# Two mixture-of-experts layers: routing from unscaled rows, modulation on VectorE, three index lists moved behind a branch

## Chip, cores and metric

The kernel runs on one core of a Trainium2 chip. The metric is the device time of one execution in microseconds; a time of several executions is given as their median.

## What is computed

The reference takes 512 tokens of 1024 floats through two blocks. The first has two layers of latent attention beside dilated attention. The second has two layers, each a mixer (attention with pooling in the first, a gated convolution in the second) and a mixture of 16 experts; each token goes to 2 of them, chosen within one of four groups. The change touches the mixture alone. Cut to what matters:

```
h = rms_norm(x, g) * (1 + scale) + shift            # "modulate"
group = top1(softmax(h @ rg_w + rg_b))
two   = top2(softmax(h @ re_w + re_b) within the group)
for e in 16 experts:
    y += weight[e] * (silu(h @ w_gate[e]) * (h @ w_up[e])) @ w_down[e]
x = x + g2 * y
```

## The kernel before

The 512 tokens lie as four tiles `x[:, i, :]` of 128 rows. `moe` is called once a layer and has four stretches.

**Routing.** The output projection of the mixer before it leaves eight half tiles of `x` open; `arrive` draws one: six matmuls (L350 to L352) and an addition on VectorE (L1037). Between them the list in the first scheduled section draws `square` (ScalarE, the sum of squares), `scaled` (L1571, `y = x * A`), `turned` (L1544, eight transpositions of `y` on TensorE, copied out by ScalarE), `logits` and `folded` (L1552, L1558), `rms` (the inverse root, a chain of one-column operations on VectorE, L384 to L397) and `modulate` (`y * rs + shift`, stored to the scratch tensor `tscr`). VectorE does `modulate` in one operation (L1582); GpSimd's form takes a scaling on ScalarE and an addition on GpSimd (L1585). Tiles 0 and 1 go to GpSimd, 2 and 3 to VectorE. `route` ranks the logits of one tile on VectorE (L1591 to L1611); `before` and `spots` turn the choice into positions within each expert.

**Index lists.** `hot` compares positions with a ramp on VectorE (L1631, tile `oh`, two buffers), `places` multiplies it with the row numbers on TensorE (L1637, L1642), `indices` adds the parts up (L1648, `ix`). `place(0, 1)` makes the list of expert 0, `place(1, 3)` those of experts 1 to 3. `fetch` (L1670) gathers the 128 rows of one expert from `tscr` with an indirect transfer that GpSimd issues.

**The branch.** A register is loaded from `over` (L1880), and every engine branches on it (L1881). The body is a loop over all experts for lists of over 128 tokens. With these inputs it isn't entered: the trace has no instruction of L1885 to L1926. Each engine passes a short other branch that waits for what stands before it on its own counters.

**Experts.** An expert multiplies the turned rows (`turn`, L1747, eight transpositions) with 1 MB of gate and up weights. Each product is three matmuls of two halves of 32 bits (`xTh`, `xTl`, `whi`, `wlo`): `split_to` makes the upper half on ScalarE (L401), the lower on VectorE or GpSimd (L402). A chunk `c1` of the weights (1024 columns) takes six matmuls, an expert 24; `hidden` (L1762) follows them, `down` the second product. `split0` makes chunks 0 to 2 of expert 0 ahead of the expert, on GpSimd. `weigh` works out the weight of each token from the logits (L1683 to L1722, 21 small operations on VectorE and two on ScalarE). `up(1)` follows `up(0)`, then the second place of `info` with the weights, then `down(0)`.

Within `manual_schedule` TensorE, GpSimd, ScalarE and VectorE take their instructions in the order in which the list is written; a scheduler lays other work between.

Of the kernel before, what the change touches and what calls it, by code (L numbers as in the profile page):

```python
# [1487 lines left out]
def router(k, L):  # L1488
# [7 lines left out]
    for c in range(8):  # L1496
# [4 lines left out]
TABLES = ("mv", "iota", "tri", "info", "rw", "fold")  # L1501
SMALL = ("lg", "sm", "cmp", "rank", "G", "lgr", "gm", "ge", "gsum", "e2", "w1", "w2", "sec", "We", "Ws",
         "Ab", "pos", "pos16", "most", "over", "oh", "row", "spread", "lgT", "ix", "ws", "vinf", "vpos", "ivx", "ivw",
# [13 lines left out]
def moe(k, L, x, tables, out):  # L1517
# [4 lines left out]
    A, sh, g2B, iota, tri, info, rw, fold = tables  # L1522
# [15 lines left out]
    def turned(i, qs=(0, 1)):  # L1538
        src = ys[i]
        tT = tTs[i] = xgs[i].rearrange("p (c t) -> p c t", c=8)  # L1540
        for q in qs:
            pt = k.bank("pt")
            for j in range(4):
                nc.tensor.transpose(pt[:, j * P : (j + 1) * P], src[:, (4 * q + j) * P : (4 * q + j + 1) * P], ident)  # L1544
            nc.scalar.activation(tT[:, 4 * q : 4 * q + 4, :], pt.rearrange("p (k t) -> p k t", k=4), AF.Copy)
# [18 lines left out]
    def square(i):  # L1564
        nc.scalar.activation(xgs[i], x[:, i, :], AF.Square, scale=float(D ** -0.5), accum_out=ss[:, i : i + 1])
# [4 lines left out]
    def scaled(i, engine, cs=slice(0, D)):  # L1570
        engine.tensor_tensor(ys[i][:, cs], x[:, i, cs], A[:, cs], ALU.mult)  # L1571
# [8 lines left out]
    def modulate(i, engine, cs=slice(0, D)):  # L1580
        if engine is v:
            v.scalar_tensor_tensor(ys[i][:, cs], ys[i][:, cs], rss[i], sh[:, cs], op0=ALU.mult, op1=ALU.add)  # L1582
        else:
            nc.scalar.activation(ys[i][:, cs], ys[i][:, cs], AF.Copy, scale=rss[i])
            engine.tensor_tensor(ys[i][:, cs], ys[i][:, cs], sh[:, cs], ALU.add)  # L1585
        if cs.stop == D:
            nc.sync.dma_start(tscr[i * P : (i + 1) * P, :], ys[i])
# [195 lines left out]
    with tc.manual_schedule(engines={ENG.PE, ENG.Pool, ENG.Activation, ENG.DVE}):  # L1783
        k.arrive()
        square(0)
        scaled(0, v)
        k.arrive()
        square(1)
        scaled(1, nc.gpsimd)
        k.arrive(1)  # L1790
        run(rms(0, 2))
        turned(0)
# [32 lines left out]
        for i in range(2):  # L1825
            before(i)
# [268 lines left out]
```

## Time and profile before

| | us |
|---|---|
| median of three runs (lowest, highest) | 1857.73 (1855.89, 1859.37) |
| the profiled execution | 1858.75 |
| its span from first to last instruction | 1857.0 |
| TensorE busy | 1705.9 (92%) |
| VectorE busy | 1346.4 (73%) |
| ScalarE busy | 770.8 (42%) |
| GpSimd busy | 278.2 (15%) |

Times in the rows are microseconds from the span's start. In the first layer of experts routing runs from 1226.5 to about 1260, the experts to about 1445. In the second routing runs from about 1625 to 1659, the experts to about 1845. The rest of the span is the attention block and the two mixers, which the change leaves as they are.

### The profile page before, as it was taken

Reading aid. Unit: us, or ns where it says so; the run is one execution under the profiler, and the core shown is the slowest. Engines: PE = TensorE matmul, PEld = TensorE weight load, DVE = VectorE, ACT = ScalarE, POOL = GpSimd, SP = SyncE. Lnnn points to the kernel's source line nnn. Section 1 sums busy time; section 2 is a strip of 40 time slices with the busy share of each in tenths; the row PEclk is TensorE's granted clock in tenths of the full one; section 3 lists DMA queues with packets and bytes.
Section 4 is the critical chain, followed back from the end, with each engine's and each line's share of the span. In section 5 each row is a group of like instructions: output and inputs, shape, how many; then the busy total and the mean of one; then the engine's idle time right before and its main releaser. Section 6 shows DMA issues by size and latency. Waiting matters only on the chain. (4 is left out here: it accounts for less than half of the span.)

```text
span 1857.0 us, 25754 instructions
## 1 busy us (share of the span) xinstructions
PE 1705.9 (92%) x9542; PEld 1334.2 (72%) x9542; DVE 1346.4 (73%) x2532; ACT 770.8 (42%) x1345; POOL 278.2 (15%) x242
## 2 busy tenths in 40 slices
PE   7999999999799999999997889987999799969996
PEld 7877777886697777778866767765666587746663
DVE  4577778876646777576677788879877765589774
ACT  4444333333343443323434445553555322145552
POOL 0000000001200000000003452023221122142221
PEclk9999999999999999999998989997999799979998
DMA  5345565664024445554413213147996463169983
GB/s 176 121 135 149 162 206 162 192 193 135 19 73 125 142 143 151 169 165 148 150 46 110 67 47 126 42 170 265 336 341 194 164 215 95 36 247 304 348 295 75
DMA packets 86948, 298.90 MB, mean 161 GB/s; under 512 B 18854, under 2 KB 20694, under 8 KB 78624
## 3 DMA queue, kind: packets, MB, share of 16 engines
q1 hardware_dynamic: 71584, 271.87, 43.8%
q0 software_dynamic: 10704, 19.79, 4.7%
q10 hardware_dynamic: 4528, 5.51, 1.1%
q8 instruction: 78, 1.28, 0.3%
q14 instruction: 54, 0.44, 0.1%
HBM read 280.23 MB, written 24.96 MB: 164 GB/s over the span
## 5 line engine op out<-in xcount | busy, mean ns | idle before, releaser
L401 ACT ACTIVATE whi<-wraw 128x1024 fp32r<-128x1024 f32 (+2 forms) x166 | 171.7, 1036 | 348.1 <-PE psmm L351 241.6
L350 PE MATMUL psmm<-big,whi 128*128 128x512 f32 x672 | 272.9, 406 | 6.8 <-DVE x L668 5.6
L402 DVE TENSOR_TENSOR wlo<-wraw,whi 128x1024 fp32r<-128x1024 f32 (+3 forms) x165 | 200.9, 1219 | 102.3 <-ACT whi L401 89.6
L352 PE MATMUL psmm<-big,wlo 128*128 128x512 f32 x672 | 266.7, 397 | 0.0
L351 PE MATMUL psmm<-big,whi 128*128 128x512 f32 x672 | 266.6, 397 | 0.0
L980 DVE CUSTOM_DVE_ANT_0 wraw<-wraw,sB 128x1024 f32<-128x1024 f32 x96 | 117.1, 1221 | 83.4 <-DMA wraw<-in_mw_dram 82.9
L350 PE MATMUL psmm<-whi,big 128*128 128x256 f32 (+2 forms) x496 | 165.1, 333 | 1.5 <-ACT big L401 1.0
L351 PE MATMUL psmm<-wlo,big 128*128 128x256 f32 (+2 forms) x496 | 160.7, 324 | 4.9 <-DVE wlo L402 4.9
L352 PE MATMUL psmm<-whi,big 128*128 128x256 f32 (+2 forms) x496 | 159.9, 323 | 2.4 <-DVE big L402 2.3
L350 PEld LDWEIGHTS psmm<-big,whi 128*128 128x128 f32 x672 | 127.3, 189 | 35.8 <-issue 4.7
L352 PEld LDWEIGHTS psmm<-big,wlo 128*128 128x128 f32 x672 | 126.9, 189 | 31.1
L351 PEld LDWEIGHTS psmm<-big,whi 128*128 128x128 f32 x672 | 127.4, 190 | 27.9
L1865 PE MATMUL psmm<-wraw,hs 128*128 128x512 f32 x256 | 122.1, 619 | 5.4 <-ACT hs L1857 3.5
L601 POOL DMA_DIRECT2D qk<-rope x40 | 20.5, 515 | 659.2 <-ACT whi L401 286.9
L351 PEld LDWEIGHTS psmm<-wlo,big 128*128 128x128 f32 x496 | 112.1, 226 | 6.2 <-DVE wlo L402 6.0
L352 PEld LDWEIGHTS psmm<-whi,big 128*128 128x128 f32 x496 | 111.5, 225 | 3.2 <-DVE big L402 3.2
L350 PEld LDWEIGHTS psmm<-whi,big 128*128 128x128 f32 x496 | 111.4, 225 | 2.7 <-ACT big L401 1.7
L350 PE MATMUL pss<-whi,xTh 128*128 128x512 f32 x256 | 104.8, 409 | 2.4 <-ACT xTh L401 2.4
L352 PE MATMUL pss<-whi,xTl 128*128 128x512 f32 x256 | 102.4, 400 | 1.7 <-DVE xTl L402 1.7
L351 PE MATMUL pss<-wlo,xTh 128*128 128x512 f32 x256 | 103.4, 404 | 0.0
L856 PEld LDWEIGHTS pspt<-c_ident,pr 128*128 128x128 f32 x512 | 61.3, 143 | 48.2 <-issue 28.9
L402 DVE TENSOR_TENSOR wlo<-bigm,whi 128x1024 fp32r<-128x1024 f32 x64 | 77.9, 1223 | 17.7 <-ACT whi L401 16.2
(384 smaller groups left out, 3659.7 us busy)
## 6 DMA issues: line engine op xcount, KB each, us to landing
wraw<-in_mw_dram SPq DMA_DIRECT2D x96, 512.0 KB
big<-in_me_dram SPq DMA_DIRECT2D x32, 1024.0 KB
bigm<-in_me_dram SPq DMA_DIRECT2D x32, 1024.0 KB
wraw<-in_me_dram SPq DMA_DIRECT2D x64, 512.0 KB
wraw<-in_wqk_dram SPq DMA_DIRECT2D x48, 512.0 KB
wraw<-in_wv_dram SPq DMA_DIRECT2D x24, 512.0 KB
wraw<-in_ow_dram SPq DMA_DIRECT2D x20, 512.0 KB
wraw<-in_wg_dram SPq DMA_DIRECT2D x16, 512.0 KB
```

Source lines behind the costliest of these rows:

```text
L350: mm(out, lhs[0], rhs[0], start=first, stop=False)
L351: mm(out, lhs[0], rhs[1], start=False, stop=False)
L352: mm(out, lhs[1], rhs[0], start=False, stop=last)
L401: self.nc.scalar.activation(hi, src, AF.Copy)
L402: (sub or self.nc.vector).tensor_tensor(lo, src, hi.bitcast(F32), ALU.subtract)
L601: nc.gpsimd.dma_start(tiles[b][48:80, :], R[b // 4][32 * (b % 4) : 32 * (b % 4) + 32, :])
L856: nc.tensor.transpose(pt[:, j * P : (j + 1) * P], hd.pr[i][:, j * P : (j + 1) * P], ident)
L980: nc.vector.tensor_tensor_reduce(w, w, sB, 1.0, 0.0, ALU.mult, ALU.add, mf[:, j : j + 1])
L1865: nc.tensor.matmul(acc, hs[:, c * P : (c + 1) * P], w[:, c * 512 : (c + 1) * 512], start=c == 0, stop=c == 1)
```

## The change

- The router's weights are scaled once (`cols`, a new small load, and one operation on VectorE), so that `turned` takes its transpositions from `x` itself and no longer from `y`.
- `scaled` and `modulate` run on VectorE alone. The tiles are modulated in the order 0, 3, 2, 1: 0 and 3 ahead of `route` of tiles 0 and 1, 2 and 1 between that and `route` of tiles 2 and 3. The squares of tile 3 are summed in two halves.
- The three `split0` go from GpSimd to VectorE and behind the branch. The scheduler lays the first of them ahead of routing.
- `place(1, 3)` and the fetch of expert 1 go from ahead of the branch to behind it. `turn`, two splits and then all of `weigh` follow.
- Two runs of idle transpositions, `warm(8)` ahead of the last two `route` and `warm(24)` between the fetch of expert 0 and the branch.
- The loads within the body of the branch go from SyncE's queue to GpSimd's.

```diff
-    tables = [brow(k, rows[L], j, ("mv", 3)) for j in (4, 3, 5)]
+    cols = small([P, 8], "cols")
+    k.nc.sync.dma_start(cols, rows[L][4:5, :].rearrange("o (c p) -> p (o c)", p=P))
+    tables = [cols] + [brow(k, rows[L], j, ("mv", 3)) for j in (4, 3, 5)]
...
-    def turned(i, qs=(0, 1)):
-        src = ys[i]
+    r3 = rw.rearrange("p (c e) -> p c e", e=32)
+    v.tensor_tensor(r3, r3, cols.unsqueeze(2).to_broadcast([P, 8, 32]), ALU.mult)
+
+    def turned(i, engines):
+
         tT = tTs[i] = xgs[i].rearrange("p (c t) -> p c t", c=8)
-        for q in qs:
+        for q, engine in enumerate(engines):
+            if engine is None:
+                continue
             pt = k.bank("pt")
             for j in range(4):
-                nc.tensor.transpose(pt[:, j * P : (j + 1) * P], src[:, (4 * q + j) * P : (4 * q + j + 1) * P], ident)
-            nc.scalar.activation(tT[:, 4 * q : 4 * q + 4, :], pt.rearrange("p (k t) -> p k t", k=4), AF.Copy)
+                c = 4 * q + j
+                nc.tensor.transpose(pt[:, j * P : (j + 1) * P], x[:, i, c * P : (c + 1) * P], ident)
+            dst, src = tT[:, 4 * q : 4 * q + 4, :], pt.rearrange("p (k t) -> p k t", k=4)
+            if engine is v:
+                v.tensor_copy(dst, src)
+            else:
+                engine.activation(dst, src, AF.Copy)
+
+    def warm(n):
+
+        pt = k.bank("pt")
+        for _ in range(n):
+            nc.tensor.transpose(pt[:, 0:P], ident, ident)
...
-    def square(i):
-        nc.scalar.activation(xgs[i], x[:, i, :], AF.Square, scale=float(D ** -0.5), accum_out=ss[:, i : i + 1])
+    sq2 = small([P, 1], "sq2")
+
+    def square(i, half=None):
+        cs = slice(0, D) if half is None else slice(half * 512, half * 512 + 512)
+        nc.scalar.activation(xgs[i][:, cs], x[:, i, cs], AF.Square, scale=float(D ** -0.5), accum_out=sq2 if half else ss[:, i : i + 1])
...
-    def scaled(i, engine, cs=slice(0, D)):
-        engine.tensor_tensor(ys[i][:, cs], x[:, i, cs], A[:, cs], ALU.mult)
+    def scaled(i, cs=slice(0, D)):
...
-    def modulate(i, engine, cs=slice(0, D)):
-        if engine is v:
-            v.scalar_tensor_tensor(ys[i][:, cs], ys[i][:, cs], rss[i], sh[:, cs], op0=ALU.mult, op1=ALU.add)
-        else:
-            nc.scalar.activation(ys[i][:, cs], ys[i][:, cs], AF.Copy, scale=rss[i])
-            engine.tensor_tensor(ys[i][:, cs], ys[i][:, cs], sh[:, cs], ALU.add)
-        if cs.stop == D:
-            nc.sync.dma_start(tscr[i * P : (i + 1) * P, :], ys[i])
+    def rms3():
+        v.scalar_tensor_tensor(ss[:, 3:4], sq2, EPS, ss[:, 3:4], op0=ALU.add, op1=ALU.add)
+        yield
+        yield from k.rsqrt_steps(ss[:, 3:4], 1, lambda rs: rss.update({3: rs}), eps=False)
+
+    def modulate(i):
+        v.scalar_tensor_tensor(ys[i], ys[i], rss[i], sh, op0=ALU.mult, op1=ALU.add)
+        nc.sync.dma_start(tscr[i * P : (i + 1) * P, :], ys[i])
...
+        act = nc.scalar
         k.arrive()
         square(0)
-        scaled(0, v)
+        scaled(0)
         k.arrive()
         square(1)
-        scaled(1, nc.gpsimd)
-        k.arrive(1)
-        run(rms(0, 2))
-        turned(0)
+        turned(0, (act, act))
+        scaled(1)
         k.arrive(1)
         logits(0)
         keep(0)
         keep(1)
-        modulate(0, nc.gpsimd)
+        run(rms(0, 2))
+        k.arrive(1)
         square(2)
-        scaled(2, v)
-        k.arrive(1)
         folded(0)
-        turned(1)
-        scaled(3, v, halves[0])
-        r2 = rms(2, 1)
-        run(islice(r2, 4))
+        turned(1, (act, act))
+        modulate(0)
         k.arrive(1)
         logits(1)
+        square(3, 0)
+        scaled(2)
+        k.arrive(1)
+        square(3, 1)
+        folded(1)
+        turned(3, (act, None))
+        scaled(3)
+        turned(3, (None, act))
+        r2 = rms(2, 1)
+        both(rms3(), r2)
+        turned(2, (act, act))
+        logits(3)
         keep(2)
         keep(3)
-        modulate(1, nc.gpsimd)
-        turned(2)
-        square(3)
-        scaled(3, v, halves[1])
-        run(r2)
-        folded(1)
-        modulate(2, v)
-        turned(3)
-        both(rms(3, 1), route(0), route(1))
-        modulate(3, v)
+        modulate(3)
+        logits(2)
+        folded(3)
+        folded(2)
+        both(route(0), route(1))
+        modulate(2)
+        modulate(1)
         if out is None:
             k.next = brow(k, k.rows[1], 1, ("mv", 3)), brow(k, k.rows[1], 0, ("mv", 3))
-        logits(2)
-        logits(3)
-        folded(2)
-        for i in range(2):
+        warm(8)
+        both(route(2), route(3))
+        for i in range(4):
             before(i)
-        folded(3)
-        for c in range(2):
-            split0(c, nc.gpsimd)
-        both(route(2), route(3))
-        before(2)
-        before(3)
         spots(0, 4)
         hot(first, pos16[:, :, 0:1], 0, 4)
         place(0, 1, 0, 2, first)
         fetch(idx[0], xgs[0])
         for j in range(4):
             second(j)
-        place(1, 3, 0, 2)
-        fetch(idx[1], xgs[1])
-        split0(2, nc.gpsimd)
         v.tensor_scalar(pos, Ab, -8192.0, 8192.0 - 256.0, op0=ALU.mult, op1=ALU.add)
         v.tensor_tensor(pos, pos, rt[:, 0:64].rearrange("p (i e) -> p i e", e=16), ALU.add)
+        warm(24)
...
-                    nc.sync.dma_start(raw, I["me"][bass.ds(ev + L * 16, 1), :, c2 * 1024 : (c2 + 1) * 1024].rearrange("o p n -> p (o n)"))
+                    nc.gpsimd.dma_start(raw, I["me"][bass.ds(ev + L * 16, 1), :, c2 * 1024 : (c2 + 1) * 1024].rearrange("o p n -> p (o n)"))
...
-        steps = weigh()
-        run(islice(steps, 5))
+        split0(0, v)
+        place(1, 3, 0, 2)
+        fetch(idx[1], xgs[1])
         xT = turn(xgs[0])
-        run(steps)
+        split0(1, v)
+        split0(2, v)
+        run(weigh())
         hm = up(0, xT)
```

**TensorE, first layer, from the branch to the first expert** (`xg_11250` and `xg_11252` are the rows of expert 0, `xg_11253` those of expert 1; `oh_11914`, `oh_11921`, `oh_11928` the comparisons for experts 1 to 3). Before:

```order
L1881 UNCONDITIONAL_BRANCH
L1747 MATMUL pspt_11919<-c_ident,xg_11250 128x128 x4
L1747 MATMUL pspt_11926<-c_ident,xg_11250 128x128 x4
L350 MATMUL pss_11949<-whi_11549,xTh_11917 128x512
L351 MATMUL pss_11949<-wlo_11550,xTh_11917 128x512
L352 MATMUL pss_11949<-whi_11549,xTl_11918 128x512
L350 MATMUL pss_11949<-whi_11549,xTh_11917 128x512
L351 MATMUL pss_11949<-wlo_11550,xTh_11917 128x512
L352 MATMUL pss_11949<-whi_11549,xTl_11918 128x512
L350 MATMUL pss_11949<-whi_11553,xTh_11917 128x512
```

and now, after the twelve rows (weights and matmuls) of `oh_11914` and `oh_11921`:

```order
L1663 LDWEIGHTS oh_11928
L1663 MATMUL psav_11260<-info_11245,oh_11928 128x2
L1768 MATMUL pspt_11941<-c_ident,xg_11252 128x128 x4
L1768 MATMUL pspt_11948<-c_ident,xg_11252 128x128 x4
L350 MATMUL pss_11984<-whi_11909,xTh_11939 128x512
L351 MATMUL pss_11984<-wlo_11910,xTh_11939 128x512
L352 MATMUL pss_11984<-whi_11909,xTl_11940 128x512
L350 MATMUL pss_11984<-whi_11909,xTh_11939 128x512
L351 MATMUL pss_11984<-wlo_11910,xTh_11939 128x512
L352 MATMUL pss_11984<-whi_11909,xTl_11940 128x512
L350 MATMUL pss_11984<-whi_11955,xTh_11939 128x512
L1768 MATMUL pspt_12020<-c_ident,xg_11253 128x128 x4
```

The matmuls of three index lists now stand between the branch and the transpositions of expert 0. In the first layer the transpositions of expert 1 follow seven matmuls of expert 0, where they followed nineteen.

**VectorE, first layer, from the branch on.** Before:

```order
L1683 TENSOR_REDUCE gm_11269<-lg_11260 128x4
L1631 TENSOR_TENSOR oh_12044<-iota_11239,pos_2391_11265 128x512
L1685 TENSOR_TENSOR ge_11270<-lg_11260,gm_11269 128x16
L1631 TENSOR_TENSOR oh_12050<-iota_11239,pos_2391_11265 128x512
L1689 TENSOR_REDUCE gsum_11271<-ge_11270 128x4
L1691 SCALAR_TENSOR_TENSOR We_11267<-sec_11266,Ab_11263 128x64
L402 TENSOR_TENSOR xTl_11918<-pspt_11919,xTh_11917 128x512
L402 TENSOR_TENSOR xTl_11918<-pspt_11926,xTh_11917 128x512
L1694 TENSOR_TENSOR We_11267<-We_11267,lg_11260 128x64
L1696 TENSOR_REDUCE e_2398_11272<-We_11267 128x4
L1700 SCALAR_TENSOR_TENSOR gsum_11271<-e_2398_11272,gsum_11271 128x4
```

and now:

```order
L1652 TENSOR_TENSOR oh_11914<-iota_11241,pos_2392_11267 128x512
L1652 TENSOR_TENSOR oh_11921<-iota_11241,pos_2392_11267 128x512
L1652 TENSOR_TENSOR oh_11928<-iota_11241,pos_2392_11267 128x512
L1652 TENSOR_TENSOR oh_12079<-iota_11241,pos_2392_11267 128x512
L1669 TENSOR_REDUCE ix_11934<-psav_11260 128x3
L1652 TENSOR_TENSOR oh_12085<-iota_11241,pos_2392_11267 128x512
L402 TENSOR_TENSOR xTl_11940<-pspt_11941,xTh_11939 128x512
L402 TENSOR_TENSOR xTl_11940<-pspt_11948,xTh_11939 128x512
L402 TENSOR_TENSOR wlo_11956<-big_11280,whi_11955 128x1024
L402 TENSOR_TENSOR wlo_11960<-big_11280,whi_11959 128x1024
L1704 TENSOR_REDUCE gm_11273<-lg_11262 128x4
L402 TENSOR_TENSOR xTl_12019<-pspt_12020,xTh_12018 128x512
```

Five comparisons and two lower halves of weights now stand ahead of `gm`, the first operation of `weigh`, and the lower half of expert 1's rows stands behind it. The third lower half of expert 0's weights follows the last operation of `weigh` in both kernels; the second layer has the same order, with expert 1's rows further down.

**VectorE, first layer, ahead of routing** (`wlo_11910` is chunk 0 of expert 0, `big` its weights):

```order
 L1037 TENSOR_TENSOR x<-psmm_11162,x 128x512
+L402 TENSOR_TENSOR wlo_11910<-big_11280,whi_11909 128x1024
+L402 TENSOR_TENSOR catl_10920<-psav_10987,cath_10919 128x512
 L1498 TENSOR_TENSOR rb_11184<-rb_11184,psmm_11188 128x20
-L402 TENSOR_TENSOR catl_10920<-psav_10987,cath_10919 128x512
```

The first lower half stands ahead of the last projection's operand `catl`.

## Rows read from the trace of the kernel before

**Rows 1.** Busy time by stretch: length, PE, PEld, DVE, ACT, POOL, granted clock, DMA.
```profile
1268.00:1273.00 5.00, 4.50 (x11) 3.55 (x12) 4.39 (x19) 2.20 (x4) 1.50 (x2) 0.53 0.96 323
1273.00:1278.00 5.00, 5.00 (x27) 4.11 (x27) 4.09 (x7) 3.81 (x5) 0.00 (x0) 1.00 0.79 279
...
1325.00:1350.00 25.00, 24.82 (x105) 17.65 (x104) 19.52 (x23) 14.85 (x19) 8.01 (x6) 1.00 0.95 333
```

**Rows 2.** Timeline of TensorE in routing: start, length, engine, line, operation, idle before.
```profile
1241.43 1.09 PE L1544 MATMUL pspt<-c_ident,y 128*128 128x128 f32 x8
...
1255.08 0.25 PE L1618 MATMUL psav<-Ab,tri 128*128 128x16 bf16 x3 [5.79 <-DVE Ab L1611]
```

**Rows 3.** Timeline of VectorE in routing, first layer.
```profile
1243.60 2.27 DVE L1571 TENSOR_TENSOR y<-x,mv 128x512 f32<-128x512 f32 x1
...
1250.30 2.41 DVE L1608 TENSOR_SCALAR G<-rank 128x4 f32<-128x4 f32 x2
...
1252.69 2.42 DVE L1611 SCALAR_TENSOR_TENSOR Ab<-rank,G 128x16 bf16<-128x16 f32 x2
1255.03 1.27 DVE L1582 SCALAR_TENSOR_TENSOR y<-y,rs_y,mv 128x1024 f32<-128x1024 f32 x1
...
1257.88 0.29 DVE L1608 TENSOR_SCALAR G<-rank 128x4 f32<-128x4 f32 x2
```

**Rows 4.** Timeline of GpSimd in routing, first layer.
```profile
1250.33 4.67 POOL L402 TENSOR_TENSOR wlo<-big,whi 128x1024 fp32r<-128x1024 f32 x2 [5.00 <-ACT whi L401]
```

**Rows 5.** Timeline, all engines, from expert 0's list to its first matmul.
```profile
1260.37 1.89 DVE L1631 TENSOR_TENSOR oh<-iota,pos 128x512 bf16<-128x512 bf16 x3
1260.40 1.65 POOL L1670 DMA_INDIRECT xg<-tscr,ix  x1 [5.40 <-DVE ix L1648]
...
1263.66 1.03 POOL L1670 DMA_INDIRECT xg<-tscr,ix  x1 [1.61 <-DVE pos L1843]
1264.23 0.17 DVE L1683 TENSOR_REDUCE gm<-lg 128x4 f32<-128x16 f32 x1 [1.08 <-DVEq L1881]
1264.34 3.29 DVE L1631 TENSOR_TENSOR oh<-iota,pos 128x512 bf16<-128x512 bf16 x1
...
1265.20 1.94 PE L1747 MATMUL pspt<-c_ident,xg 128*128 128x128 f32 x8 [2.61 <-DMA xg<-tscr,ix]
...
1267.87 1.07 ACT L401 ACTIVATE xTh<-pspt 128x512 fp32r<-128x512 f32 x2
...
1268.50 0.80 PE L350 MATMUL pss<-whi,xTh 128*128 128x512 f32 x1 [1.36 <-ACT xTh L401]
```

**Rows 6.** Timeline of VectorE and TensorE beside expert 0, first layer.
```profile
1267.55 0.16 DVE L1685 TENSOR_TENSOR ge<-lg,gm 128x16 f32<-128x16 f32 x1
...
1268.48 1.29 DVE L402 TENSOR_TENSOR xTl<-pspt,xTh 128x512 fp32r<-128x512 f32 x2
...
1273.20 1.22 DVE L402 TENSOR_TENSOR wlo<-big,whi 128x1024 fp32r<-128x1024 f32 x1
...
1273.75 0.39 PE L352 MATMUL pss<-whi,xTl 128*128 128x512 f32 x1
1273.98 0.39 PE L350 MATMUL pss<-whi,xTh 128*128 128x512 f32 x1
```

**Rows 7.** Timeline of ScalarE: ends of the matmuls of experts 0 and 1, first layer.
```profile
1276.80 0.39 ACT L1762 ACTIVATE pr<-pss 128x256 f32<-128x256 f32 x1 [0.34 <-PE pss L352]
...
1283.71 0.38 ACT L1762 ACTIVATE pr<-pss 128x256 f32<-128x256 f32 x1 [0.25 <-PE pss L352]
```

**Rows 8.** Transfers into xg from 1255 to 1290, issue to landing.
```profile
DMA to landing us min/median/max: 4.8/8.1/8.3
```

**Rows 9.** Timeline of the second layer: fetch of expert 0, first matmul, end of expert 1.
```profile
1658.98 1.62 POOL L1670 DMA_INDIRECT xg<-tscr,ix  x1 [5.58 <-DVE ix L1648]
...
1665.62 0.79 PE L350 MATMUL pss<-whi,xTh 128*128 128x512 f32 x1
...
1681.96 0.38 ACT L1762 ACTIVATE pr<-pss 128x256 f32<-128x256 f32 x1 [0.33 <-PE pss L352]
```

More of the change, by code (lines that the diff above doesn't have):

```diff
@@ L1498, in router @@
     nc.vector.tensor_tensor(rb, rb, shift, ALU.add)
-TABLES = ("mv", "iota", "tri", "info", "rw", "fold")
+TABLES = ("mv", "cols", "iota", "tri", "info", "rw", "fold")
 SMALL = ("lg", "sm", "cmp", "rank", "G", "lgr", "gm", "ge", "gsum", "e2", "w1", "w2", "sec", "We", "Ws",
-         "Ab", "pos", "pos16", "most", "over", "oh", "row", "spread", "lgT", "ix", "ws", "vinf", "vpos", "ivx", "ivw",
+         "Ab", "pos", "pos16", "most", "over", "oh", "row", "spread", "lgT", "ix", "ws", "vinf", "vpos", "ivx", "ivw", "sq2",
          "rs_v2", "rs_y2", "rs_h2", "rs_u2")
@@ L1521, in moe @@
     small = lambda shape, nm, dt=F32: t(shape, nm, 1, dt)
-    A, sh, g2B, iota, tri, info, rw, fold = tables
+    cols, A, sh, g2B, iota, tri, info, rw, fold = tables
     rb = k.rb
@@ L1562, in folded @@
             lgs[i] = lgr[:, i, :]
-    def square(i):
-        nc.scalar.activation(xgs[i], x[:, i, :], AF.Square, scale=float(D ** -0.5), accum_out=ss[:, i : i + 1])
+    sq2 = small([P, 1], "sq2")
+    def square(i, half=None):
+        cs = slice(0, D) if half is None else slice(half * 512, half * 512 + 512)
+        nc.scalar.activation(xgs[i][:, cs], x[:, i, cs], AF.Square, scale=float(D ** -0.5), accum_out=sq2 if half else ss[:, i : i + 1])
     def keep(i):
         nc.sync.dma_start(xbuf[i * P : (i + 1) * P, :], x[:, i, :])
-    def scaled(i, engine, cs=slice(0, D)):
-        engine.tensor_tensor(ys[i][:, cs], x[:, i, cs], A[:, cs], ALU.mult)
+    def scaled(i, cs=slice(0, D)):
+        v.tensor_tensor(ys[i][:, cs], x[:, i, cs], A[:, cs], ALU.mult)
     def rms(i, n):
@@ L1918, in moe @@
                     o0 = 4096 + n * 1024
-                    nc.sync.dma_start(raw, I["me"][bass.ds(ev + L * 16, 1), :, o0 : o0 + 1024].rearrange("o p n -> p (o n)"))
+                    nc.gpsimd.dma_start(raw, I["me"][bass.ds(ev + L * 16, 1), :, o0 : o0 + 1024].rearrange("o p n -> p (o n)"))
                     acc = k.bank("mm")
```

## The prediction

> **What bounds the kernel now.** Read first the busy time by stretch. Once the experts run, TensorE is busy 24.82 of 25 us [rows 1]: nothing but its own matmuls sets the pace there, so what an expert loses at the start is still missing at the end. The two places where TensorE is not the bound lie in routing, once in each layer, and there the timelines of the single engines tell who is late.
>
> In the first layer TensorE stands idle 5.79 us until VectorE has written `Ab` [rows 2]. VectorE in turn looks busy throughout, but not with work of its own: a pair of one-column operations at L1608 takes 2.41 us where the same pair later takes 0.29, and L1611 2.42 us [rows 3]. Both lie beside GpSimd's two splits, 4.67 us from 1250.33 on [rows 4]. Another case is `scaled`, 2.27 us for 512 columns where `modulate` takes 1.27 us for 1024 columns [rows 3], and `oh` behind the branch, 3.29 us against 0.63 us each in the run of three [rows 5]. So the trace shows that VectorE comes to a halt beside GpSimd's wide operations.
>
> From the list of expert 0 on it is another chain: the fetch is issued at 1260.40, TensorE waits for the gathered rows until 1265.20, ScalarE copies them at 1267.87 behind `ge`, which the halted `oh` made late, and the first matmul starts at 1268.50 [rows 5]. Its clock is then at the lower level, 1.2 GHz: a granted clock of 0.53, eleven matmuls in 4.50 us or 0.41 us each, until 1.00 is granted in the next stretch [rows 1] and they follow each other in 0.23 us [rows 6].
>
> **The sum, for one layer after the other.** I split each into three stretches: up to the fetch of expert 0; from there to the first matmul; from there to the end of expert 1, behind which TensorE sets the pace.
>
> *Up to the fetch.* With GpSimd silent, L1608 and L1611 give back 2.1 us each and `scaled` 1.6 us (2.27 less half of 1.27), 5.8 us in all. Against that VectorE has one more `modulate` behind the last half tile (three where there were two), 1.27 us, half a `scaled` more, 0.64 us, and the root of tile 3 no longer laid between the routes: some ten operations of about 0.1 to 0.2 us, of which I take 1 us. That leaves 2.9 us of gain. The stores of tiles 2 and 1 now go out one right behind the other ahead of the fetch that reads them; what the second costs has no row of its own, and I take 0.6 us, between nothing and a third of the 4.8 us of a fetch [rows 8], nearer to nothing since two routes lie between. Gain 2.3 us; the ends are 5.8 (all that is added hidden) and 0 (VectorE waits for ScalarE's squares and TensorE's logits as it waited for GpSimd). That the transpositions take `x` lets them start earlier, but TensorE idles behind them anyway [rows 2]: nothing. The scaling of the router's weights is one operation, no longer than an `oh`, 0.63 us [rows 5], in the mixer before: nothing; uncovered it would cost that once. `split0(0)` stands ahead of the projection and needs weights asked for long before; it costs a wide split, 1.22 us [rows 6], only if those were late.
>
> *From the fetch to the first matmul.* Before: 8.10 us (1260.40 to 1268.50) [rows 5], in the second layer 6.64 (1658.98 to 1665.62) [rows 9]. Then the gathering hid the other lists and the branch. Now TensorE runs 24 idle transpositions, takes the branch, makes three lists, and only then turns expert 0's rows; the gathered rows, 4.8 us after the issue at best [rows 8], are there by then. Transpositions: 0.14 us each at full clock (1.09 for 8) [rows 2], 0.24 at the lower level (1.94 for 8) [rows 5]: 3.3 to 5.8 us, I take 4.6. Branch: no less than VectorE's 1.08 us, no more than TensorE's whole wait of 2.61 us [rows 5]; I take 1.5. Three lists: three `oh` of 0.63 and the last matmuls, 2.2 us; VectorE can't start them early, since the order puts them behind its own branch and the buffer of the first is free only when TensorE is through the branch. Four transpositions 0.55 to 1.0 and half of ScalarE's copy, 0.54 us [rows 5]. Less 0.5 us, by which expert 0's matmuls precede the issue. Together 9.1 us (7.2 to 12), that is 1.0 us more in the first layer, 2.5 us more in the second.
>
> *From the first matmul to the end of expert 1.* Before: 15.21 us (to 1283.71) [rows 7], 16.34 in the second layer [rows 9]. `weigh` ran while TensorE made those first slow matmuls, and the third lower half, 1.22 us, followed at 1273.20 [rows 6], 4.7 us after the first matmul. Now VectorE begins `weigh` only behind two `xTl` (1.29 us) and two lower halves (2.44). Fetch 1 is issued at the end of the lists, some 1.6 us ahead of the first matmul, and lands 4.8 to 8.1 us later [rows 8], 3.2 to 6.5 us after the first matmul. In the first layer TensorE needs those rows after seven matmuls, 1.6 to 2.9 us: a wait of 0.3 to 4.9 us, and `weigh` stops there too, since `xTl` of expert 1 stands within it. Then: rows turned and copied, 1.1 to 1.5 us; `xTl`, 1.3 us in two parts; `weigh`, 3.7 us (from `ge` at 1267.55 to 1273.20, less the 1.29 of `xTl` and one `oh`); the third lower half 1.22; five matmuls 1.2. The end of expert 0 comes 12 to 15.5 us after the first matmul, where it came 8.3 us after it [rows 5, 7]. Expert 1 then needs at least its 23 other matmuls, 5.3 us, at most the 6.9 us of before [rows 7]. Together 17.5 to 22.3, I take 19.2: 4.0 us more. In the second layer TensorE needs the rows after eighteen matmuls, which hides the landing; the same chain gives 18.8 (17.5 to 20.5): 2.5 us more.
>
> The sums are -2.3 + 1.0 + 4.0 = 2.7 us and -2.3 + 2.5 + 2.5 = 2.7 us. **Both layers: 5.4 us slower**, 1864.2 against the profiled execution's 1858.75. The median of the runs is 1.0 us below that execution, so against it I give **1863**.
>
> Off the path: ScalarE loses four scalings. The loads in the branch's body change nothing, as the body isn't run. What remains of that edit is the other branch of GpSimd, which then waits for all its transfers, the fetch of expert 0 among them. It lands 4.8 us after the issue; GpSimd's next task, fetch 1, isn't due before the branch and the lists, 7 us or more after it. Uncovered, it would move fetch 1 back one for one.
>
> **Two rules weighed.** The fetches behind the branch took 1.03 us to issue while VectorE was idle at the branch [rows 5]; the trace of before has none beside the splits that now stand there. The Trainium skill ("SBUF — State Buffer", section "SBUF: two separate sides") says that VectorE's operations on two ports keep GpSimd from writing the descriptors of its own transfers. By that rule, which no row here shows, fetch 1 could come a comparison or a split later, and the sum would be about 1 us higher in each layer.
>
> The second is the clock. The rows show TensorE idle for 5.79 us [rows 2] and a clock of 0.53 some us later [rows 1]. The Trainium skill ("TensorE: Matmul & The Clock Gate", section "What's actually happening") says that the clock follows how busy the engine has been lately. The trace agrees as far as it goes; by that rule the idle transpositions would bring expert 0 the full clock, which is the first rival.
>
> **Rivals.**
> - *Faster: the clock.* Place: the 24 transpositions. If the higher level, 2.4 GHz, is granted from early on in them, the second stretch takes 7.6 us (-0.5 and +1.0), and if VectorE's chain doesn't end expert 0, the third is TensorE's own 48 matmuls, 24 transpositions and the small ones: 14 us (-1.2 and -2.3). With -2.3 each: -7.6 us, 1850. It decides at one point: the third lower half must be ready 8 us after the first matmul. For it speaks the halt of 5.8 us, which surely goes; against it VectorE's order, whose pieces add up to over 10 us there.
> - *Much slower: fetch 1.* It shares the engines with the weights of expert 0's second product. At 8.1 us [rows 8] and the lower clock throughout, the second stretch takes 11.5 us, the third 22.3 and 20.5: 8.2 and 6.8 us, together 15 us, 1873.
> - *No difference.* The gain in routing is 4 us in place of 2.3, and the rest as in the sum: +2.0 us, 1860. The other branch of this: edits that change only a branch not taken, and idle work, of which nothing arrives.
>
> **How the numbers follow.** Forecast 0.44, faster 0.18, no difference 0.22, much slower 0.16. A change within 0.2% (3.7 us), about what a measurement of this kernel tells from none, is 'same'. The forecast's own range is 1861.5 to 1868. The range of 8 in 10 reaches halfway into both outer rivals: 1853 to 1873. Faster 0.18, same 0.22, slower 0.60.
>
> **What would show it.** Right: L1608 and L1611 short, no wait of 5.79 us, GpSimd without a wide operation in routing; expert 0's end 12 us or more after its first matmul; a wait of TensorE for `xg` of expert 1 in the first layer alone; the third lower half behind `weigh`, late. Wrong: a first matmul over 3 us earlier in the layer's own time, a clock of 1.00 under it, or an end of expert 1 no more than 16 us behind it.

## The result, and the profile after the change

| | before | after |
|---|---|---|
| median, us | 1857.1 | 1867.0 |
| lowest to highest | 1853.98 to 1859.37 | 1862.88 to 1873.12 |
| ratio, 95% interval | | 1.0057 [1.0038, 1.0076] |
| profiled execution, its span | 1858.75, 1857.0 | 1862.88, 1860.9 |

The change costs 9.9 us by the medians. The profiled pair differs by 4.1 us only, because routing of the first layer begins 6.0 us earlier in the span of after: in the attention block and the first mixer, which the change leaves alone. In the other executions of this study that point lies anywhere from 1217 to 1227 us (at 1218.6 in e6, the kernel before with one small tile more). So the layers are compared from a point of their own, a small product that both kernels make shortly before routing (the router's shift, the start of L1497). TensorE's timeline there, both layers, before and then after:

```profile
1224.72 1.96 PE L1497 MATMUL psmm<-rws,mod 128*128 128x20 f32 x16
...
1609.04 1.86 PE L1497 MATMUL psmm<-rws,mod 128*128 128x20 f32 x16
```

```profile
1218.71 1.96 PE L1497 MATMUL psmm<-rws,mod 128*128 128x20 f32 x16
...
1610.08 1.86 PE L1497 MATMUL psmm<-rws,mod 128*128 128x20 f32 x16
```

| us from that point | layer 1 before | after | layer 2 before | after |
|---|---|---|---|---|
| fetch of expert 0 issued | 35.68 | 32.33 | 49.94 | 46.34 |
| fetch of expert 1 issued | 38.94 | 39.30 | 52.62 | 54.16 |
| first matmul of expert 0 | 43.78 | 39.63 | 56.58 | 53.55 |
| its matmuls end (`hidden`) | 52.08 | 58.09 | 64.72 | 68.23 |
| those of expert 1 end | 58.99 | 63.70 | 72.92 | 74.38 |
| those of expert 3 end | 82.49 | 87.94 | 95.70 | 100.15 |
| those of expert 15 end | 212.86 | 219.96 | 227.58 | 231.95 |

Both layers reach the first matmul earlier, 4.2 and 3.0 us, and have lost all of that and more two experts later: +4.7 and +1.5 us. These are single executions. The kernel before repeats its two columns within 0.2 us (e11); the second layer of the change does not: with addresses alone altered (e5) expert 1 ends there 2.0 us later, at 76.37.

One name first. Expert 0 has four chunks of weights, so four lower halves. `split0` makes those of chunks 0 to 2; what the change's description and the prediction call the third one, behind `weigh`, is that of the last chunk, which `up` makes. Below it is the last lower half.

**Routing.** Timeline of VectorE, TensorE and GpSimd in routing of the first layer, after (start, length, engine, line, operation, idle before):

```profile
1243.51 0.29 DVE L1629 TENSOR_SCALAR G<-rank 128x4 f32<-128x4 f32 x2
1243.70 0.30 DVE L1632 SCALAR_TENSOR_TENSOR Ab<-rank,G 128x16 bf16<-128x16 f32 x2
1243.92 2.48 DVE L1607 SCALAR_TENSOR_TENSOR y<-y,rs_y,mv 128x1024 f32<-128x1024 f32 x2
...
1248.39 0.30 PE L1639 MATMUL psav<-Ab,tri 128*128 128x16 bf16 x5 [4.09 <-DVE Ab L1632]
...
1251.04 1.11 POOL L1691 DMA_INDIRECT xg<-tscr,ix  x1 [93.02 <-DVE pos L1859]
```

The pairs that took 2.41 and 2.42 us [rows 3] take 0.29 and 0.30; GpSimd has done nothing for 93.02 us when it issues the fetch, where it had two splits [rows 4]. TensorE still waits, 4.09 us against 5.79 [rows 2], now for two `modulate` that stand between the routes.

**From the fetch on, first layer.** The same view, after:

```profile
1249.86 4.34 PE L1563 MATMUL pspt<-c_ident 128*128 128x128 f32 x24
...
1254.47 2.50 DVE L1652 TENSOR_TENSOR oh<-iota,pos 128x512 bf16<-128x512 bf16 x4 [3.58 <-PEq L1898]
...
1256.56 1.95 PE L1768 MATMUL pspt<-c_ident,xg 128*128 128x128 f32 x8
...
1258.01 1.03 POOL L1691 DMA_INDIRECT xg<-tscr,ix  x1 [5.86 <-PE pspt L1768]
1258.34 0.79 PE L350 MATMUL pss<-whi,xTh 128*128 128x512 f32 x1
...
1260.12 2.36 DVE L402 TENSOR_TENSOR wlo<-big,whi 128x1024 fp32r<-128x1024 f32 x2 [0.25 <-ACT whi L401]
1262.39 0.16 DVE L1704 TENSOR_REDUCE gm<-lg 128x4 f32<-128x16 f32 x1
...
1266.61 1.51 PE L1768 MATMUL pspt<-c_ident,xg 128*128 128x128 f32 x6 [5.71 <-DMA xg<-tscr,ix]
...
1268.37 0.69 DVE L402 TENSOR_TENSOR xTl<-pspt,xTh 128x512 fp32r<-128x512 f32 x1 [5.82 <-ACT xTh L401]
1268.98 0.17 DVE L1706 TENSOR_TENSOR ge<-lg,gm 128x16 f32<-128x16 f32 x1
...
1274.05 3.49 DVE L402 TENSOR_TENSOR wlo<-big,whi 128x1024 fp32r<-128x1024 f32 x3
...
1275.32 0.50 PE L351 MATMUL pss<-wlo,xTh 128*128 128x512 f32 x1 [0.73 <-DVE wlo L402]
...
1276.80 0.39 ACT L1783 ACTIVATE pr<-pss 128x256 f32<-128x256 f32 x1 [2.42 <-PE pss L352]
1282.41 0.39 ACT L1783 ACTIVATE pr<-pss 128x256 f32<-128x256 f32 x1 [0.44 <-PE pss L352]
```

Read it as one chain. The idle transpositions hold TensorE, and VectorE waits 3.58 us for TensorE's queue at the branch before it may make the lists. Behind them fetch 1 goes out at 1258.01. TensorE makes seven matmuls of expert 0 and then stands 5.71 us in front of expert 1's rows; VectorE has done `gm` and stands with it, because `xTl` of expert 1 lies within `weigh`. Only then comes the rest of `weigh`, and behind it the last lower half at 1274.05, 15.7 us after the first matmul; before it was 4.7 us [rows 6].

**Second layer.** The same view, after:

```profile
1656.42 1.07 POOL L1691 DMA_INDIRECT xg<-tscr,ix  x1 [56.49 <-DVE pos L1859]
...
1663.63 0.79 PE L350 MATMUL pss<-whi,xTh 128*128 128x512 f32 x1
...
1671.20 1.07 PE L1768 MATMUL pspt<-c_ident,xg 128*128 128x128 f32 x8 [1.69 <-DMA xg<-tscr,ix]
...
1674.50 3.49 DVE L402 TENSOR_TENSOR wlo<-big,whi 128x1024 fp32r<-128x1024 f32 x3
...
1684.46 0.38 ACT L1783 ACTIVATE pr<-pss 128x256 f32<-128x256 f32 x1 [0.44 <-PE pss L352]
```

Here TensorE needs the rows after eighteen matmuls and waits 1.69 us; the last lower half comes 10.9 us after the first matmul, the end of expert 1 after 20.8, where it was 16.3 [rows 9].

**Clock.** Busy time by stretch, after (columns as in [rows 1]):

```profile
1249.00:1254.00 5.00, 4.43 (x29) 4.27 (x29) 1.56 (x10) 0.00 (x0) 1.11 (x1) 0.60 0.74 227
...
1253.00:1256.40 3.40, 1.76 (x22) 1.40 (x20) 1.93 (x4) 0.00 (x0) 0.00 (x0) 1.00 0.42 96
1256.40:1259.80 3.40, 3.37 (x16) 2.81 (x17) 2.57 (x5) 1.86 (x3) 1.49 (x2) 0.50 0.74 220
...
1261.00:1266.50 5.50, 0.00 (x0) 0.00 (x0) 1.56 (x3) 0.03 (x1) 1.20 (x1) 0.70 0.70 249
1266.50:1270.00 3.50, 3.39 (x11) 3.00 (x12) 1.30 (x5) 0.82 (x2) 0.00 (x0) 0.50 0.21 85
1270.00:1275.00 5.00, 2.93 (x19) 1.91 (x17) 4.19 (x16) 3.64 (x5) 0.00 (x0) 0.99 0.00 0
...
1700.00:1705.00 5.00, 3.99 (x33) 2.78 (x32) 5.00 (x11) 1.09 (x2) 2.60 (x2) 0.86 1.02 403
1705.00:1711.00 6.00, 6.00 (x36) 4.76 (x34) 4.18 (x6) 3.95 (x6) 0.00 (x0) 0.84 0.83 238
```

The idle transpositions end at 1254.20 with the higher level granted (1.00). It is lost again, first under expert 0's turn and first matmuls (0.50 from 1256.4 on), then behind the wait of 5.71 us, where the granted clock is again 0.50, the lower level. The last two rows lie at expert 3 of the second layer.

### The profile page after: what moved, and what is told of

Same layout as the page of the kernel before. It is cut to its first block, busy times and chain, and to the rows that moved or that the text cites. A ratio compares the mean times of both kernels' runs of the same rounds, so it can differ in the third digit from the quotient of the medians.

```text
span 1860.9 us, 25854 instructions
## 1 busy us (share of the span) xinstructions
PE 1713.7 (92%) x9606; PEld 1339.0 (72%) x9606; DVE 1343.0 (72%) x2544; ACT 766.1 (41%) x1345; POOL 251.4 (14%) x230
## 5 line engine op out<-in xcount | busy, mean ns | idle before, releaser
L402 DVE TENSOR_TENSOR wlo<-wraw,whi 128x1024 fp32r<-128x1024 f32 (+3 forms) x165 | 202.1, 1227 | 98.3 <-ACT whi L401 86.3
L601 POOL DMA_DIRECT2D qk<-rope x40 | 20.5, 514 | 657.8 <-DVE pr L798 165.5
L402 DVE TENSOR_TENSOR wlo<-big,whi 128x1024 fp32r<-128x1024 f32 x64 | 77.9, 1224 | 20.1 <-ACT whi L401 19.8
```

The source lines that it names most:

```text
L402: (sub or self.nc.vector).tensor_tensor(lo, src, hi.bitcast(F32), ALU.subtract)
L601: nc.gpsimd.dma_start(tiles[b][48:80, :], R[b // 4][32 * (b % 4) : 32 * (b % 4) + 32, :])
```

## Experiments

Two explanations compete. In the texts of e1 and e3 "fetch 1 is late" is the theory and VectorE's order behind the branch (lists, two lower halves, then `weigh`, then the last one) its rival; after e3 the order is the theory. Two further suspects: the loads' queue, which holds GpSimd at its branch, and the idle transpositions. Each is undone alone, then some together. Differences are to the kernel before in the same set of runs, whose medians were 1855.3 (e1 to e4), 1856.5 (e5 to e8) and 1857.4 (e9 to e12).

**e1: the lists and fetch 1 back ahead of the branch.**

```diff
             second(j)
+        place(1, 3, 0, 2)
+        fetch(idx[1], xgs[1])
...
         split0(0, v)
-        place(1, 3, 0, 2)
-        fetch(idx[1], xgs[1])
```

> The changed kernel with one part undone: the lists of experts 1 to 3 and the fetch of expert 1 stand ahead of the branch again, between the second choices and the idle transpositions. Theory (fetch 1 is late): in the trace of the changed kernel TensorE waits 5.71 us in the first layer and 1.69 us in the second for the rows of expert 1, and expert 0 ends 18.5 and 15 us after its first matmul. With the fetch some 7 us earlier both waits go, the first matmul comes no later (2 us of lists move under the gathering), and the end of expert 1 comes 5 to 8 us earlier in the first layer, 2 to 4 us in the second: about 8 us below the changed kernel, level with or below the kernel before. Rival (VectorE's order): the two lower halves and the whole of the weights still stand ahead of the third lower half, expert 0 still ends over 12 us after its first matmul, and no more than 3 us come back.

1870.2 us, ratio 1.008 [1.0063, 1.0098]: nothing comes back, where the theory expected about 8 us. It is no clean test of the first layer: there the fetch itself stayed behind GpSimd's branch, 39.28 us from the layer's point as in the change (39.30), and expert 1 ended later, at 66.65 in place of 63.70. In the second it went out at 48.98 in place of 54.16, the wait for the rows was gone, and expert 1 still ended at 74.21, as good as unmoved from 74.38.

**e2: the loads of the branch's body back on SyncE's queue.**

```diff
-                    nc.gpsimd.dma_start(raw, ...
+                    nc.sync.dma_start(raw, ...
```

> The changed kernel with one part undone: the loads in the body of the branch are on SyncE's queue again. Theory: GpSimd's other branch then no longer waits for the landing of fetch 0 (4.1 us in the trace of the changed kernel) before its 1.2 to 1.8 us instruction on the queue's counter, so fetch 1 is issued right behind its list, 1.0 us earlier in the first layer and 1.5 us in the second, and TensorE's wait for it shrinks by as much: 1 to 2.5 us below the changed kernel. Rival (the body isn't run, so its queue is nothing to the time): fetch 1 at the same distance behind its list, the wait unchanged, no difference.

1866.2 us, ratio 1.0066 [1.0045, 1.0087]: no difference from the change. Fetch 1 went out 0.3 and 1.1 us earlier, less than the theory's 1.0 and 1.5.

**e3: the three lower halves of `split0` on VectorE, but ahead of the branch.**

```diff
         warm(24)
+        split0(0, v)
+        split0(1, v)
+        split0(2, v)
...
-        split0(0, v)
         place(1, 3, 0, 2)
...
-        split0(1, v)
-        split0(2, v)
```

> The changed kernel with one part moved: the three halvings of expert 0's first weights stand ahead of the branch, still on ScalarE and VectorE, where VectorE idles 3.6 us beside the idle transpositions. Lists and fetch 1 stay behind the branch. Theory (fetch 1 is late): in the first layer the wait of 5.7 us stays, since the seven matmuls in front of it need no further half, and the end of expert 1 moves by under 1.5 us; in the second layer the wait of 1.7 us grows by what is gained in front of it. Together 0 to 3 us below the changed kernel. Rival (VectorE's order): the 2.4 us of halvings are gone from the chain in both layers, 4 to 6 us come back.

1856.7 us, ratio 1.001 [0.9997, 1.0023]: level with the kernel before, some 8 us of the 9.9 are back, more than either side expected. Timeline of VectorE and TensorE of this run, first layer:

```profile
1252.37 3.49 DVE L402 TENSOR_TENSOR wlo<-big,whi 128x1024 fp32r<-128x1024 f32 x3
...
1261.38 0.16 DVE L1704 TENSOR_REDUCE gm<-lg 128x4 f32<-128x16 f32 x1
...
1265.88 1.22 DVE L402 TENSOR_TENSOR wlo<-big,whi 128x1024 fp32r<-128x1024 f32 x1
...
1268.35 1.94 PE L1768 MATMUL pspt<-c_ident,xg 128*128 128x128 f32 x8 [3.08 <-DMA xg<-tscr,ix]
```

The three halves run while VectorE had waited at the branch. `weigh` follows `xTl` at once. The scheduler now also lays expert 1's transpositions behind nineteen matmuls, so part of the gain in the first layer (4.9 us by the end of expert 1) is TensorE's order; in the second, where the halves alone moved it, it is 2.6 us. What is left is a wait for expert 1's rows, 3.08 us in the first layer and 2.25 in the second.

**e4: no `warm(24)`.** The edit takes that line out.

> The changed kernel without the 24 idle transpositions. They take 4.3 us in each layer, and the lists behind the branch wait for TensorE to be through them. Theory (they only delay): the lists start about 3 us earlier in each layer, up to what the landing of fetch 0 allows the first matmul; fetch 1 is issued 2 to 3 us earlier, while the first matmul gains 0 to 2 us, and the end of expert 1 comes 1.5 to 3 us earlier in each layer: 3 to 6 us below the changed kernel. Rival (they keep the clock): expert 0 then starts at a granted clock of 0.5 as in the kernel before, its first matmuls take 0.43 us each in place of 0.23, and what is gained in front is lost there: no difference or slower.

1869.9 us, ratio 1.008 [1.0058, 1.0103]: no gain. VectorE at the branch in the first layer of this run, TensorE's branch instruction there (by source line, lengths in ns), and fetch 1 in the second layer:

```profile
1257.31 2.50 DVE L1652 TENSOR_TENSOR oh<-iota,pos 128x512 bf16<-128x512 bf16 x4 [3.50 <-PEq L1897]
...
L1897 PEldq COMPARE_BRANCH  x1: 2695/2695/2695, 1254.5 to 1254.5; - x1
...
1670.49 1.03 POOL L1691 DMA_INDIRECT xg<-tscr,ix  x1 [7.49 <-ACT xTh L401]
```

In the first layer VectorE waits as long as with the transpositions, 3.50 us for 3.58, since TensorE's branch instruction alone takes 2.69 us there (2.33 in the change, 0.37 in the second layer of both). So the lists and the first matmul come no earlier (39.53 against 39.63). In the second layer the lists do come earlier, by 3.2 us, but TensorE then waits 3.08 us for expert 0's rows; GpSimd waits at its branch for the same landing (4.82 us), so fetch 1 goes out 5.5 us behind its finished list; and expert 1's transpositions follow seven matmuls, not eighteen. Expert 0 ends at 73.66 in place of 68.23. e2 has no such wait of GpSimd, so the loads' queue holds back here what the missing transpositions free, and e4 is no clean test of them. Why expert 0's rows took 5.67 us to land (4.92 in the change) was not tried.

**e5 to e8: addresses, and the whole order.** The trace shows one loss that no part of the sum had: from expert 5 on, an expert takes 10.49 and 10.48 us in the two layers after, but 10.35 us in the first layer before (10.49 in the second). Ends of the matmuls of experts 5 and 11 on ScalarE's timeline, before and then after:

```profile
1329.70 0.38 ACT L1762 ACTIVATE pr<-pss 128x256 f32<-128x256 f32 x1 [0.30 <-PE pss L352]
...
1391.78 0.38 ACT L1762 ACTIVATE pr<-pss 128x256 f32<-128x256 f32 x1 [0.30 <-PE pss L352]
```

```profile
1329.37 0.38 ACT L1783 ACTIVATE pr<-pss 128x256 f32<-128x256 f32 x1 [0.34 <-PE pss L352]
...
1392.31 0.38 ACT L1783 ACTIVATE pr<-pss 128x256 f32<-128x256 f32 x1 [0.34 <-PE pss L352]
```

62.08 and 62.94 us for six experts. Averaged over 60 to 80 neighbouring matmuls, one starts 0.227 us after the other there and 0.233 in every other layer looked at. What had changed was where tiles lie in SBUF: `cols` and `sq2` push `xTh`, the rows of an expert, 64 bytes further.

**e5: `sq2` wider.**

> The changed kernel with nothing but sq2 made wider (17 columns in the first layer, 25 in the second), so that every tile behind it, xTh among them, lies on an address that is a multiple of 128 bytes, as xTh did in the first layer of the kernel before alone. Theory 'addresses' (the two new small tiles moved xTh from 177792 to 177856, and the spacing of matmuls followed): 0.2275 us from matmul to matmul in place of 0.233, 10.35 us an expert in place of 10.48 in both layers, about 2 us less in each, 1863 us. Theory 'something else sets the spacing' (the order of VectorE, the transfers): 10.48 us an expert in both layers, 1867 us, no difference from the changed kernel.

```diff
-    sq2 = small([P, 1], "sq2")
+    sq2 = small([P, 17 if out is None else 25], "sq2")
...
```

1870.7 us, ratio 1.0088 [1.0064, 1.0112], and 10.47 us an expert in both layers: a multiple of 128 bytes isn't what counts.

**e6: the kernel before with a small tile ahead of `xTh`.**

> The kernel before with nothing but a 64-byte tile ahead of xTh (xTh at 177856 in the first layer, as in the changed kernel; 175776 in the second, which was off a multiple of 128 before as well). Theory 'addresses': the first layer goes from 10.35 to 10.48 us an expert, the second stays at 10.49; 2 us slower, 1859 us. Rival: 10.35 in the first layer as before and no difference, 1857 us.

```diff
+    pad = small([P, 16], "pad")
+    v.memset(pad, 0.0)
```

The first layer went to 10.49 us an expert, as expected. The time did not show it: 1855.9 us, ratio 1.0006 [0.9991, 1.0022], an interval that also takes in the 2 us.

**e7: the edits of e3 and e5 together.**

> The two edits together: the three lower halves of expert 0 on VectorE ahead of the branch, and sq2 wide. The first alone measured 1856.7. Theory 'addresses': 2 us less in each layer, 1852.7, faster than the kernel before by 2 to 4 us; 10.35 us an expert in both layers. Rival: 1856.7, level with the kernel before.

1854.3 us, ratio 0.9994 [0.9977, 1.0011]; 10.47 us an expert, so e5's answer again. Level with the kernel before, and not told apart from e3.

**e8: lists, fetch 1 and the three `split0` ahead of the branch, `weigh` round `turn`.** The wide `sq2` of e5 and the queue of e2 are in this run too, beside what is printed below.

> As the run before this one, and besides the three index lists and the fetch of expert 1 ahead of the lower halves, ahead of the branch; weigh round turn as in the kernel before; the loads of the branch's body on SyncE's queue, so that GpSimd passes its other branch without waiting. Theory 'VectorE's order and a late fetch 1': with the splits gone from behind the branch, fetch 1 is now what TensorE waits for (3.08 us with the splits moved alone); it goes out some 3 us earlier, the wait goes, the end of expert 1 comes 16 us or less behind the first matmul in both layers (19.2 and 18.8 with the splits alone), 3 us less a layer: 1847, faster than the kernel before by 8 to 10 us. Rival 'VectorE is the bound, not fetch 1': the lists ahead of the splits only change who waits; the end of expert 1 stays 18 to 19 us behind the first matmul, 1853.

```diff
             second(j)
+        place(1, 3, 0, 2)
+        fetch(idx[1], xgs[1])
...
+        split0(0, v)
+        split0(1, v)
+        split0(2, v)
         warm(24)
...
-        split0(0, v)
-        place(1, 3, 0, 2)
-        fetch(idx[1], xgs[1])
+        steps = weigh()
+        run(islice(steps, 5))
         xT = turn(xgs[0])
-        split0(1, v)
-        split0(2, v)
-        run(weigh())
+        run(steps)
```

1849.5 us, ratio 0.9965 [0.9948, 0.9982]: faster than the kernel before by 7 us and 4.8 below e7, where 3 us a layer were expected. Timeline of GpSimd, VectorE and TensorE of this run, first layer:

```profile
1256.40 1.11 POOL L1691 DMA_INDIRECT xg<-tscr,ix  x1 [93.06 <-SPq L1903]
...
1258.52 3.49 DVE L402 TENSOR_TENSOR wlo<-big,whi 128x1024 fp32r<-128x1024 f32 x3
...
1259.72 2.06 POOL L1691 DMA_INDIRECT xg<-tscr,ix  x1 [2.22 <-DMA qk<-rope]
...
1264.99 0.50 PE L350 MATMUL pss<-whi,xTh 128*128 128x512 f32 x1 [0.25 <-ACT xTh L401]
...
1269.77 0.71 PE L1768 MATMUL pspt<-c_ident,xg 128*128 128x128 f32 x5
1270.97 0.50 PE L351 MATMUL pss<-wlo,xTh 128*128 128x512 f32 x1 [0.49 <-DVE wlo L402]
```

Fetch 1 goes out 3.3 us after fetch 0 (7.0 in the change) and TensorE turns expert 1's rows without a wait. Expert 1 ends 14.4 and 15.6 us after the first matmul, where the kernel before had 15.2 and 16.3. From e7 to e8 `weigh` and the queue change along with fetch 1; what each gives was not tried alone.

**e9: e8 without `warm(24)`.**

> The run e8 (lists, fetch 1 and lower halves ahead of the branch, sq2 wide; 1849.5) without the 24 idle transpositions, which there stand behind the lists on TensorE and ran from 1257.91 to 1263.27, up to the transpositions of expert 0's rows. Theory 'they cost what they delay': the first matmul comes when the rows are in, some 7 us after the fetch in place of 8.6, 1 to 1.5 us earlier a layer, and the clock under it at the lower level as in the kernel before, which gives 1 to 2 us back: 1848 to 1850, no difference. Rival 'they bring the clock': without them the first dozen matmuls take 0.41 us each in place of 0.23, 2 us more a layer and nothing gained, since the rows land no earlier: 1853.

1847.3 us, ratio 0.9938 [0.9915, 0.9962]: not told apart from e8. Both effects are in the trace and nearly cancel. The first matmul comes 0.9 and 1.2 us earlier (40.04 for 40.95, 53.27 for 54.47); eight and eleven steps from matmul to matmul then take about 0.43 us, and expert 0 ends 0.15 us earlier than in e8 in the first layer and 0.6 us later in the second.

**e10: e8 with `sq2` of 504 and 512 columns.**

> The run e8 with sq2 wider still (504 and 512 columns), so that xTh lies at 177792 in the second layer, exactly where the kernel before has it in its first, and at 179840, a multiple of 2048 bytes further, in the first. Theory 'the address of xTh sets the spacing of matmuls': 0.2275 us and 10.35 us an expert in the second layer, in the first too if what counts repeats within 2048 bytes; 2 to 4 us faster than e8, 1846 to 1848. Rival 'not the address': 0.233 us and 10.47 us an expert in both layers, 1849.5.

1846.8 us, ratio 0.994 [0.9919, 0.9961], the fastest median of all, 3.6 us below e8 by the difference to the kernel before, though the intervals touch. The trace is plain: 10.37 us an expert in both layers, a start every 0.228 us. Ends of experts 5 and 11, first layer:

```profile
1326.31 0.39 ACT L1783 ACTIVATE pr<-pss 128x256 f32<-128x256 f32 x1 [0.30 <-PE pss L352]
...
1388.51 0.39 ACT L1783 ACTIVATE pr<-pss 128x256 f32<-128x256 f32 x1 [0.30 <-PE pss L352]
```

62.20 us, close to the 62.08 before the change. At 0.106 us an expert (10.473 less 10.367) it is 1.5 us a layer. So the spacing is shown; that the time follows it is not, here as in e6.

**e11: the kernel before again.**

> The kernel before once more, for a second profiled execution. If the spacing belongs to the program (addresses, order), the first layer has 10.35 us an expert again and the second 10.49. If it belongs to the execution, the two layers come out otherwise than they did, and the 2.4 us that the changed kernel loses from expert 2 to expert 15 are no part of what the change costs.

1858.6 us, ratio 1.0001 [0.998, 1.0022]; 10.35 and 10.49 us an expert, as the first time. The spacing belongs to the program.

**e12: e1 and e2 together.**

> The changed kernel with the three lists and the fetch of expert 1 ahead of the branch and the body's loads on SyncE's queue, the two edits of e1 and e2 together; the lower halves and weigh stay behind the branch, in the change's order. In both layers fetch 1 then goes out about 3 us behind fetch 0, which neither edit did alone in the first layer. Theory 'VectorE's order': the two lower halves and weigh are still ahead of the third one; the end of expert 1 stays 19 us or more behind the first matmul, 1862 to 1866, slower than the kernel before. Rival 'fetch 1 and the lists behind the branch are the cost': the waits for its rows go, the end of expert 1 comes 16 us behind the first matmul, 1855 to 1857.

1861.7 us, ratio 1.002 [1.0006, 1.0035]: 4.3 us slower than before, so about half of the 9.9 is back. Expert 1 ends 19.5 us after the first matmul in both layers, as the theory had it; the time is at the lower edge of its 1862 to 1866. Timeline of GpSimd, TensorE and VectorE, first layer:

```profile
1252.97 1.03 POOL L1691 DMA_INDIRECT xg<-tscr,ix  x1 [2.21 <-DVEq L1900]
...
1257.38 0.50 PE L350 MATMUL pss<-whi,xTh 128*128 128x512 f32 x1 [0.25 <-ACT xTh L401]
...
1259.37 0.82 PE L1768 MATMUL pspt<-c_ident,xg 128*128 128x128 f32 x6
...
1267.16 3.49 DVE L402 TENSOR_TENSOR wlo<-big,whi 128x1024 fp32r<-128x1024 f32 x3
1268.44 0.79 PE L351 MATMUL pss<-wlo,xTh 128*128 128x512 f32 x1 [0.73 <-DVE wlo L402]
```

The wait for expert 1's rows is gone, and TensorE waits for the last lower half all the same: behind `weigh`, 9.8 us after the first matmul. So VectorE's order costs with an early fetch 1 too; and once the halves are moved, TensorE waits for the late fetch (3.08 us in e3), a wait that is gone in e8. Moving the halves alone is worth about 8 us, the early fetch 1 with the queue about 6. e8, which has both and `weigh` round `turn` besides, is 17 us below the change: the two add up, and the 3 us beyond their sum are within what these intervals leave open.

## Why the prediction was right, and where its steps were off

Forecast: 1863 us, slower. Measured: 1867.0, within the range, slower. The forecast's mechanism held; its sizes partly did not. That they came this close is in part luck: two stretches were forecast too dear and one too cheap, and 3.7 us of the 9.9 came from behind the last stretch, where the sum had nothing.

- **Up to the fetch:** a gain of 2.3 us was taken; 3.35 and 3.6 were measured, near the 4 us of the rival 'No difference'. The halts of the first layer went as told; if all 5.8 us came back, the costs set against them were put 1 us too high.
- **From the fetch to the first matmul:** 9.1 us was taken; 7.3 and 7.2 were measured, at the lower end of 7.2 to 12. Transpositions: 4.34 us for 4.6. The branch was the wrong term: 1.5 us, where VectorE begins the lists 0.27 us behind the last idle transposition (1254.47 against 1249.86 + 4.34): the branch ran beside them (TensorE's own took 2.33 us, from 1252.0 on). So the second stretch won 0.8 us in the first layer where 1.0 was to be lost, and lost 0.6 in the second where 2.5 was.
- **From there to the end of expert 1:** 19.2 and 18.8 us were taken; 24.1 and 20.8 were measured, above both ranges (22.3 and 20.5 at most). This is the term that was mis-sized. The pieces were named rightly: wait for the rows, `weigh` stopped within, the last half behind. But the wait was given 0.3 to 4.9 us and was 5.71. Fetch 1 was to go out 1.6 us ahead of the first matmul; it went out 0.3 us ahead (0.6 us behind it in the second layer), and its rows took 8.5 us to land where 8.1 was the most. From the end of the wait to the end of expert 0 it then took 10.2 us where the pieces come to 8.5 to 8.9: the lower clock behind the wait was not in the sum. In the second layer the landing was taken as hidden and cost 1.69 us.
- **The sum to there:** +2.7 a layer was taken; +4.7 and +1.5 were measured. 5.4 against 6.2 us.
- **"TensorE's own matmuls set the pace" from then on:** this step failed as it was put. They do set it, but the pace changed: 2.4 us more from expert 2 to expert 15 in the first layer, 1.7 of it by the spacing. In the second layer, 3.0 us more were lost between the ends of experts 1 and 3 (25.8 for 22.8). About half goes with the clock, which fell to 0.84 to 0.86 at expert 3: e5, the same order without that fall, takes 24.2 there. The rest goes with the order, in which two matmuls of expert 0's second product now lie behind the end of expert 1. The layers' ends are 7.1 and 4.4 us late; 1.6 us less in the second mixer and behind the last expert stand against that. That makes 9.9 us for this pair, without the earlier start of the profiled execution.
- **The rival 'clock'** fell: in the change the clock was at the lower level again under expert 0's first matmuls and behind the wait (0.50); in e8, where expert 0's rows follow them at once, the matmuls follow each other in 0.23 us from the fourth on. Even so they brought no time (e9). **The rival 'fetch 1'** had the right wait, and its third stretch of 22.3 and 20.5 us was even exceeded, but its 15 us were too many: the second stretch took 7.3 and 7.2 us, not 11.5. **'Off the path: the loads in the body'** held by time (e2), though GpSimd did wait there for the landing of fetch 0, and fetch 1 could not use an early list without that edit undone (e1 against e12).
- **The rule on GpSimd's descriptors** was to cost fetch 1 a comparison or a split. In the changed kernel it did not: fetch 1 took 1.03 us. A longer issue shows elsewhere: beside the three lower halves it takes 2.06 us (e8, 1259.72), against 1.03 in e12 where VectorE waits. The Trainium skill ("SBUF — State Buffer", section "SBUF: two separate sides") says that GpSimd cannot write descriptors while VectorE runs an operation on two ports; these rows agree, though none shows which ports the halves use.

## What to carry to other kernels

An operation is cheap or dear by what stands behind it on its in-order engine: with expert 0's halvings behind the branch the kernel takes some 8 us more than with the same halvings ahead of it, where VectorE was waiting anyway. So before moving work from one engine to another, look for a wait there that can take it, and keep whatever releases the next transfer (here the index lists) ahead of it. And when a new tile goes in, compare the steady pace of loops that the change doesn't touch.

## What was not expected of the hardware

The start-to-start time of the same matmuls depends on where their operands lie in SBUF: 0.227 to 0.228 us with `xTh` at 177792 (before, first layer; e10, second) or 179840 (e10, first), 0.233 with it at 175712, 175776, 175872, 177856 or 177920 (before, second layer; after and e6; e5, e7 and e8). The fast addresses are equal modulo 2048 and the slow ones differ from them; a multiple of 128 is not enough. All tiles behind `sq2` move with `xTh`, so which operand counts, and by what step, stays open.
